# A two-layer decoder trunk on one core: sums of halves moved from GpSimd to VectorE, vectors and masks made at the start, a shared port in the emission's model

## The chip, the cores and the metric

One NeuronCore of a Trainium2 chip runs the whole kernel. The metric is device time in microseconds of one execution. TensorE (PE) multiplies matrices, VectorE (DVE), ScalarE (ACT) and GpSimd (POOL) work elementwise, and SyncE (SP) issues nearly all the DMAs. Each engine runs its own instructions strictly in the order in which they were written, and waits at the first one whose inputs aren't there.

## The reference

`x` is 512 tokens by 1024 features in float32. Each of two layers is a half-weighted SwiGLU feed-forward part, a mixer of two branches, and a second feed-forward part:

```python
for l in range(DEPTH):                                   # DEPTH = 2
    x = x + 0.5 * swiglu(rmsnorm(x, n1[l]), w_in1[l], w_out1[l])   # d_ff = 2816
    x = x + hybrid_mixer(rmsnorm(x, nm[l]), ...)
    x = x + 0.5 * swiglu(rmsnorm(x, n2[l]), w_in2[l], w_out2[l])

def swiglu(h, w_in, w_out):
    gate, up = jnp.split(h @ w_in, 2, axis=-1)
    return (jax.nn.silu(gate) * up) @ w_out
```

The mixer projects `h` onto the inputs of branch A (a gated DeltaNet of 8 heads: short convolution, chunks of 64 tokens with a triangular solve, and a state carried from chunk to chunk) and of branch B (stick-breaking attention of 8 heads), and onto gates. Both branches go through their own 1024x1024 projection, are gated, added, and projected by `w_out`.

## The kernel before, in words

Everything is kept transposed, features on partitions, 512 tokens along the free axis. Matmuls run in float32r with each operand split into a high and a low part: ACT makes the high part of a weight chunk (`wh`), DVE the low part (`wl<-raw,wh`), and a product is three matmuls, high by high, low by high and high by low (`mm3`). An ordinary projection gives matmuls named `pf`.

**Feed-forward part.** The first four column units of the hidden layer ("c" in the `PLAN`) are ordinary products. The rest is made in nine quads ("s"): a quad takes four weight blocks b11, b21, b22, b12 and forms seven products of halves instead of eight. For that each quad needs four sums of weight blocks (`sums` and `last_sum`: in the trace `s<-sraw`, `sraw<-sraw` twice, and `sraw<-s,sraw`, each 128x1024), and the part needs, once, four sums of halves of the normalised activations `xs` (`halves`: `sx<-xs` twice, `xs<-xs`, `sx<-xs,sx`). All of these run on GpSimd. Each sum is the raw form of one further weight operand, so ACT and DVE then split it (`wl<-sraw`, `wl<-s`; `th`, `tl<-sx`). The down projection ("d", matmuls `pf<-hp`) stands between the quads; its first columns come ahead of quad 0. `hp` is the split hidden activation. Split weights live in rings of four buffers in this part (three in the mixer), so a new one can be made when PE is through with the oldest.

**Mixer.** A string `ORDER` says which projection comes when (D and S for the branches, G and Z for gates, B for the projection of branch B, E for the end of the first stage). The DeltaNet runs in four pairs of heads. A pair is a chain: scores, a blocked inverse (`pp`, `pt`), then four rounds over the tokens (`dn_recur`: PE `pa`, DVE `rhs`, PE `py`, ACT `y` and `yw`, PE `po`, DVE `s`), then the norm of the heads (`dn_out`: `osq`, `dsc`, scaling on ACT, transposes `oT` on PE). Such chains are put in between the matmuls of projections, so that PE has work while it waits for the other engines.

**What sets the order.** The program is emitted by Python code in which a model (`Weave`, with a cost for each engine, `COST`) keeps a clock. After each projection matmul `tick` lets every chain whose inputs the model holds to be ready emit its next step. `idle(engine)` puts a step off while the model's engine is busy, `until` runs chains up to a condition, and `drain` runs all of them out. The order that results on PE, ACT, DVE and POOL is final. At "E" `drain` runs whatever chain is left, with no projection matmul between its steps.

**The start.** `load_x` loads x in five DMAs, transposes it block by block (`xps`, into a ring of three PSUM buffers with the tag "dp", which `vp` and `adt_ps` share), and starts the first two column units. Only the gain of the first norm is loaded ahead of x (`column`). All other vectors per feature (`vt`, turned by a transpose `vp` and a copy), the row of decay parameters (`adt_row`, spread by the matmul `adt_ps`) and the masks are made by `more_constants`, a chain that is released 20 us (model time) later and must be done before quad 0.

Of the kernel before, what the change touches and what calls it, by code (L numbers as in the profile page):

```python
# [74 lines left out]
class Weave:  # L75
# [13 lines left out]
    def __init__(self, nc):  # L89
        self.t = 0.0  # L90
        self.cur = 0.0
        self.free = dict.fromkeys(("vector", "scalar", "gpsimd", "sync", "dma"), 0.0)
        self.writes = {}
# [38 lines left out]
    def charge(self, engine, op, outs, ins, func=None):  # L132
# [20 lines left out]
        else:  # L153
# [182 lines left out]
class Trunk:  # L336
# [46 lines left out]

    def column(self, name, ap):
        for _ in self.columns(name, ap):
            pass

    def columns(self, name, ap):

        nc = self.nc  # L390
        rows = ap.shape[0]
        dst = self.cst.tile([P, rows], F32, name="v_" + name)
        for r0 in range(0, rows, P):
            n = min(P, rows - r0)
            t = self.stat.tile([P, P], F32, tag="sq", bufs=SQ, name="vt")
            nc.scalar.dma_start(t[:n, :], ap[r0:r0 + n, :])
            yield self.weave.landed(t)
            ps = self.dps.tile([P, SEQ], F32, tag="dp", name="vp")
            nc.tensor.transpose(ps[:, :n], t[:n, :], self.ident[:n, :n])
            nc.vector.tensor_copy(dst[:, r0:r0 + n], ps[:, :n])  # L400
        self.vcol[name] = dst

    def constants(self):
        nc = self.nc
        self.vcol = {}
        self.ident = self.select("ident", ALU.is_equal, 0, 1, -1)
        self.ones = self.cst.tile([P, P], F32, name="ones")
        nc.gpsimd.memset(self.ones, 1.0)
        self.eps = self.cst.tile([P, 1], F32, name="eps")
        nc.gpsimd.memset(self.eps, EPS)  # L410

    def more_constants(self, vecs, a_log, dt_bias):
        nc = self.nc
        c = self.cst
        for name, ap in vecs:
            yield from self.columns(name, ap)
            yield 1000
        t = self.stat.tile([P, P], F32, tag="sq", bufs=SQ, name="gt")
        self.select("gt", ALU.is_gt, 0, 1, -1, out=t)
        self.m_gt = c.tile([P, P], F32R, name="m_gt")  # L420
        nc.scalar.copy(self.m_gt, t)
        self.m_le = self.select("m_le", ALU.is_ge, 0, -1, 1)
# [12 lines left out]
        yield 2000  # L435

        n = DEPTH * HEADS
        row = c.tile([1, 2 * n], F32, name="adt_row")
        nc.scalar.dma_start(row[:, 0:n], a_log.rearrange("(o l) h -> o (l h)", o=1))
        nc.scalar.dma_start(row[:, n:2 * n], dt_bias.rearrange("(o l) h -> o (l h)", o=1))  # L440
        yield self.weave.landed(row)
        ps = self.dps.tile([P, SEQ], F32, tag="dp", name="adt_ps")
        nc.tensor.matmul(ps[:, :2 * n], self.ones[0:1, :], row, start=True, stop=True)
# [3 lines left out]
        nc.scalar.activation(self.nea, self.adt[:, 0:n], AF.Exp)  # L447
        nc.vector.tensor_scalar(self.nea, self.nea, -1.0, None, op0=ALU.mult)
        self.sbg = c.tile([P, DEPTH], F32, name="sbg")
# [11 lines left out]

    def load_x(self, x, gain):

# [3 lines left out]
        with self.pool("xin", 1) as xin:  # L467
            self.column(*gain)
# [75 lines left out]
    def finish_norm(self):  # L544

        nc = self.nc
        nc.scalar.preload_act_table_set("natural_log_exp_and_others")
        ps = self.dps.tile([P, SEQ], F32, tag="dp", name="ssps")
        nc.tensor.matmul(ps, self.ones, self.ssq, start=True, stop=True)
        y = self.stat.tile([P, SEQ], F32, tag="r", name="r")  # L550
        tmp = self.stat.tile([P, SEQ], F32, tag="sq", bufs=SQ, name="rtmp")
        nc.scalar.activation(tmp, ps, AF.Ln, scale=1.0 / D, bias=self.eps[:, 0:1])
        nc.scalar.activation(y, tmp, AF.Exp, scale=-0.5)
        nc.vector.tensor_scalar(tmp, ps, 1.0 / D, EPS, op0=ALU.mult, op1=ALU.add)
        nc.vector.tensor_mul(tmp, tmp, y)
# [231 lines left out]
    def sums(self, q):  # L787
# [9 lines left out]
        nc.gpsimd.tensor_tensor(t[21], t[11], t[21], op=ALU.subtract)  # L797
        f.events.add("s3")
        yield 0
        while 1 not in f.events:  # L800
            yield 300
        nc.gpsimd.tensor_tensor(t[11], t[0], t[11], op=ALU.subtract)
        f.events.add("s2")
        yield 0

    def last_sum(self, q):
        f, t = self.fours[q], self.fours[q].tiles
        while not f.events >= {2, "s2"}:
            yield 300
        self.nc.gpsimd.tensor_tensor(t[12], t[12], t[11], op=ALU.subtract)  # L810
        f.events.add("s4")
# [3 lines left out]
    def halves(self, hid):  # L815
# [60 lines left out]
    def ffn(self, hid, w_in, w_out, finish, first=None):  # L876
# [127 lines left out]
        for item in PLAN:  # L1004
            if item[0] == "d" and later is None:
# [721 lines left out]
def hybrid_trunk(ctx, tc, x, ffn1_norm, ffn1_w_in, ffn1_w_out, mix_norm, w_in, dn_conv_w, dn_a_log,  # L1727
# [9 lines left out]
    def gains(name, l):  # L1737
# [3 lines left out]
        mybir.EngineType.PE, mybir.EngineType.Activation, mybir.EngineType.DVE, mybir.EngineType.Pool}))  # L1741
    T.constants()
    T.begin_norm(gains("n1", 0))
    first = T.load_x(x[0], ("n1", rows(ffn1_norm)))
    T.weave.spawn(T.weave.after("constants", T.more_constants([
        ("nm", rows(mix_norm)), ("n2", rows(ffn2_norm)),
        ("conv", dn_conv_w.rearrange("l t (k p) -> (l t k) p", p=P)),
        ("dno", dn_out_norm), ("sbq", sb_q_norm), ("sbk", sb_k_norm),
    ], dn_a_log, dn_dt_bias)), 20000)

# [49 lines left out]
```

## Time and profile before

| | us |
|---|---|
| median of 3 runs (2808.15 to 2808.47) | 2808.41 |
| the profiled execution | 2805.78 |
| its span (first to last instruction) | 2803.9 |
| PE busy | 2750.8 |
| DVE busy | 1998.8 |
| ACT busy | 1466.4 |
| POOL busy | 681.7 |

The span is what the trace covers; 1.9 us of the profiled execution lie around it. Times in the rows are counted from the span's start. A row of a timeline has start, duration, engine, line of the helper that issued it, operation, output and inputs, shapes, count, and in brackets how long the engine had been idle and what released it. All instructions go through one helper, so the line is always the same and rows are told apart by the names of their tiles. "PEclk" is TensorE's granted clock as a share of 2.4 GHz.

### The profile page before, as it was taken

What the parts mean: (1) busy time and instruction counts of PE and PEld (TensorE: products, weight loads), DVE (VectorE), ACT (ScalarE), POOL (GpSimd) and SP (SyncE); (2) the same over time, 40 slices, a digit from 0 to 9 for tenths busy, and PEclk for the clock granted to TensorE, in tenths of its full rate; (3) what the DMA queues carried; (4) which work ended last, traced back from release to release, by engine and by line L of the source; (5) the groups of instructions that cost most, each with busy time, mean ns of one, the idle gap of its engine ahead of it and who ended that gap; (6) DMA issues with size and microseconds to landing.
All of it is one profiled execution on the core that took longest, in us unless ns stands there. A gap on an engine that the chain in (4) does not pass through costs nothing.

```text
span 2803.9 us, 44397 instructions
## 1 busy us (share of the span) xinstructions
PE 2750.8 (98%) x17230; PEld 2441.1 (87%) x17230; DVE 1998.8 (71%) x2994; ACT 1466.4 (52%) x2955; POOL 681.7 (24%) x400
## 2 busy tenths in 40 slices
PE   8999999999999999999999999999999999999999
PEld 6899988888888887999979999889988888889998
DVE  6877576986787556867578675778878765588664
ACT  4544346767664544534445344468675745445333
POOL 5444120100100044523145341210001002355330
PEclk9999999999999999999999999999999999999999
DMA  5333143322335654333143331323323358433332
GB/s 152 102 106 105 49 123 89 95 78 83 96 97 180 222 170 134 102 100 112 50 132 97 103 116 56 113 81 86 102 80 96 104 158 291 137 95 106 102 94 64
DMA packets 438034, 312.47 MB, mean 111 GB/s; under 512 B 31562, under 2 KB 408128, under 8 KB 437824
## 3 DMA queue, kind: packets, MB, share of 16 engines
q1 hardware_dynamic: 437488, 309.51, 36.9%
q8 instruction: 135, 2.21, 0.3%
q14 instruction: 75, 0.61, 0.1%
q10 hardware_dynamic: 336, 0.13, 0.0%
HBM read 276.03 MB, written 33.55 MB: 110 GB/s over the span
## 4 chain that ended last, share of the span: by engine, by line
PE 79%; DVE 10%; issue 4%; ACT 3%; POOL 2%; DMA 1%; SPq 0%; DVEq 0%; POOLq 0%; ACTq 0%
PE pf L279 51%; PE pq L279 15%; PE ps L279 7%; DVE wl L279 3%; ACT u L279 1%; DVE itmp L279 1%; DVE sbs L279 1%; PE sbo_ps L279 1%; DVE qkv L279 1%; POOL t L279 1%; DVE it L279 1%; PE z_ps L279 1%; PE pa L279 1%; PE at_ps L279 0%; PE pp L279 0%
## 5 line engine op out<-in xcount | busy, mean ns | idle before, releaser
L279 DVE TENSOR_TENSOR wl<-raw,wh 128x1024 fp32r<-128x1024 f32 (+2 forms) x351 | 430.8, 1228 | 138.4 <-ACT wh L279 135.7
L279 ACT ACTIVATE wh<-raw 128x1024 fp32r<-128x1024 f32 (+2 forms) x352 | 336.9, 959 | 300.6 <-PE pf L279 149.9
L279 PE MATMUL pf<-xh,wl 128*128 128x512 f32 (+1 forms) x1312 | 486.1, 371 | 5.3 <-DVE wl L279 5.3
L279 PE MATMUL pf<-xh,wh 128*128 128x512 f32 (+1 forms) x1312 | 487.0, 371 | 0.2 <-DVE t L279 0.2
L279 PE MATMUL pf<-xl,wh 128*128 128x512 f32 (+1 forms) x1312 | 486.7, 371 | 0.0
L279 PE MATMUL pf<-hp,wh 128*128 128x512 f32 x1408 | 439.3, 392 | 2.1 <-DVE hp L279 1.1
L279 DVE TENSOR_TENSOR wl<-sraw,wh 128x1024 fp32r<-128x1024 f32 x216 | 377.3, 1757 | 64.3 <-ACT wh L279 64.3
L279 PEld LDWEIGHTS pf<-hp,wh 128*128 128x128 f32 x1408 | 264.6, 189 | 58.3 <-DVE hp L279 2.2
L279 ACT ACTIVATE wh<-sraw 128x1024 fp32r<-128x1024 f32 x216 | 228.3, 1057 | 133.7 <-PE pf L279 102.1
L279 PEld LDWEIGHTS pf<-xh,wl 128*128 128x128 f32 x1312 | 248.0, 189 | 48.1 <-DVE wl L279 8.9
L279 PE MATMUL pf<-hp,wl 128*128 128x512 f32 x704 | 276.0, 392 | 7.6 <-DVE wl L279 7.6
L279 PEld LDWEIGHTS pf<-xl,wh 128*128 128x128 f32 x1312 | 248.0, 189 | 39.1 <-issue 1.2
L279 PEld LDWEIGHTS pf<-xh,wh 128*128 128x128 f32 x1312 | 248.0, 189 | 38.6 <-issue 1.1
L279 POOL TENSOR_TENSOR sraw<-sraw 128x1024 f32<-128x1024 f32 x72 | 212.2, 2963 | 246.1 <-DVE wl L279 189.9
L279 PE MATMUL pq<-th,wh 128*128 128x256 f32 x864 | 244.9, 283 | 3.0 <-ACT u L279 3.0
L279 PE MATMUL pq<-th,wl 128*128 128x256 f32 x864 | 244.6, 283 | 0.3 <-DVE wl L279 0.3
L279 PE MATMUL pq<-tl,wh 128*128 128x256 f32 x864 | 244.5, 283 | 0.0
L279 PE MATMUL pf<-wh,xh 128*128 128x256 f32 x768 | 225.3, 293 | 0.0
L279 PE MATMUL pf<-wl,xh 128*128 128x256 f32 x768 | 217.3, 283 | 0.0
L279 PE MATMUL pf<-wh,xl 128*128 128x256 f32 x768 | 216.9, 282 | 0.0
L279 DVE SCALAR_TENSOR_TENSOR x<-pf,x 128x512 f32<-128x512 f32 x128 | 87.7, 687 | 156.9 <-PE pf L279 156.7
L279 PEld LDWEIGHTS pq<-th,wh 128*128 128x128 f32 x864 | 165.8, 192 | 3.9 <-ACT u L279 3.8
(1090 smaller groups left out, 6275.3 us busy)
## 6 DMA issues: line engine op xcount, KB each, us to landing
sraw<-in_ffn_w_in_dram SPq DMA_DIRECT2D x144, 512.0 KB, 3.6
raw<-in_w_in_dram SPq DMA_DIRECT2D x144, 512.0 KB, 3.9
raw<-in_ffn_w_out_dram SPq DMA_DIRECT2D x96, 384.0 KB, 3.4
raw<-in_ffn_w_in_dram SPq DMA_DIRECT2D x32, 512.0 KB, 3.9
raw<-in_ffn_w_out_dram SPq DMA_DIRECT2D x32, 256.0 KB, 2.8
gsp<-gt SPq DMA_DIRECT2D x32, 256.0 KB, 2.7
of<-osp SPq DMA_DIRECT2D x32, 256.0 KB, 3.9
raw<-in_w_branch_b_dram SPq DMA_DIRECT2D x16, 512.0 KB, 4.0
```

What stands on the lines that cost most here:

```text
L279: return f(*args, **kw)
```

## The change

Four things are changed.

1. The 144 sums of weight blocks and the 16 sums of halves of activations are issued on VectorE. Ahead of each, `idle("vector", ...)` is asked.
2. `constants` issues all loads of vectors at once, ahead of x: five from ACT's queue (16, 128, 64, 16 and 16 rows of 128), five from POOL's (the three small vectors and the two halves of `adt_row`), and then makes the masks on POOL. Behind block 1 of x, `load_x` now has two transposes, one copy, the matmul `adt_ps` and its copy, `sbg`, and ACT's copy of one mask. The gate before quad 0 is gone, and one small exponential is made in the first `finish_norm`.
3. The model knows a port that VectorE (operations with two wide inputs in SBUF) and GpSimd (with one or more) share: such an operation starts when the port is free, and holds it to its end. As this model sets the order of everything, the whole program is emitted in another order.
4. `finish_norm` waits 800 ns of model time before it emits the sum over features (`ssps`).

```diff
@@ class Weave, charge
-            end = self.free[engine] = max(self.free[engine], need) + fixed + per * n
+            wide = sum(a.space != bass.MemoryType.PSUM and m > 1 for a, m in zip(ins, sizes[len(outs):]))
+            start = max(self.free[engine], need)
+            if wide >= {"vector": 2, "gpsimd": 1}.get(engine, 9):
+                start = max(start, self.port)
+                self.port = start + fixed + per * n
+            end = self.free[engine] = start + fixed + per * n
@@ constants
+        for group in (vecs[:1], vecs[1:]):
...
+                    (nc.scalar if rows > 2 else nc.gpsimd).dma_start(
+                        tiles[at // P][at % P:at % P + m, :], ap[r:r + m, :])
...
+        nc.gpsimd.dma_start(self.adt_row[:, 0:n], a_log.rearrange("(o l) h -> o (l h)", o=1))
+        nc.gpsimd.dma_start(self.adt_row[:, n:2 * n], dt_bias.rearrange("(o l) h -> o (l h)", o=1))
@@ load_x
+            self.turn_vectors()
             for k in range(KD + 4):
+                if k == 2:
+                    self.turn_vectors()
+                    self.more_constants()
@@ finish_norm
+        yield 800
         ps = self.dps.tile([P, SEQ], F32, tag="dp", name="ssps")
@@ sums, last_sum (each of the four)
-        nc.gpsimd.tensor_tensor(t[0], t[21], t[22], op=ALU.add)
+        yield from self.weave.idle("vector", LO_WAIT)
+        nc.vector.tensor_tensor(t[0], t[21], t[22], op=ALU.add)
@@ halves
-            nc.gpsimd.tensor_tensor(raw[i], a, b, op=ALU.subtract)
+            yield from self.weave.idle("vector", 1500)
+            nc.vector.tensor_tensor(raw[i], a, b, op=ALU.subtract)
@@ ffn
-            if item == ("s", 0, 1):
-                self.weave.until(lambda: self.weave.done("constants"))
```

At the start of the program PE's order before was this (`vp` turns the first gain, each `xps` group is a block of x, `pf` the first column unit):

```order
L279 MATMUL vp<-ident,vt 128x16
L279 MATMUL xps<-ident,xin_116 128x128 x4
L279 MATMUL xps<-ident,xin_118 128x128 x4
L279 MATMUL xps<-ident,xin_122 128x128 x4
L279 MATMUL pf<-xh,wh 128x512
```

and it is now:

```order
L285 MATMUL vp<-ident,vt 128x16
L285 MATMUL xps<-ident,xin_141 128x128 x4
L285 MATMUL xps<-ident,xin_143 128x128 x4
L285 MATMUL vp<-ident,vt 128x128
L285 MATMUL vp<-ident,vt 128x102
L285 MATMUL adt_ps<-adt_row,ones 128x32
L285 MATMUL xps<-ident,xin_147 128x128 x4
L285 MATMUL pf<-xh,wh 128x512
```

Two transposes and `adt_ps` have moved ahead of block 2 of x. Later in the same part the single `vp` and `adt_ps` matmuls between the `pf<-hp` are gone.

At the start of the second feed-forward part of layer 0, around the first columns of the down projection, VectorE's order before was this (`wl<-raw` 128x512 are the weights of those columns, `tl<-sx` splits the sums that POOL had made, `t` and `hp` belong to the last column unit):

```order
L279 TENSOR_TENSOR hp<-t,hp 128x512
L279 TENSOR_TENSOR wl<-raw,wh 128x512
L279 TENSOR_TENSOR t<-pf,r 128x512
L279 TENSOR_TENSOR tl<-sx,th 128x1024
L279 TENSOR_TENSOR wl<-raw,wh 128x512
L279 TENSOR_TENSOR tl<-sx,th 128x1024
L279 TENSOR_TENSOR t<-pf,t 128x512
L279 TENSOR_TENSOR tl<-sx,th 128x1024
L279 TENSOR_TENSOR hp<-t,hp 128x512
```

and it is now:

```order
L285 TENSOR_TENSOR sraw<-sraw 128x1024
L285 TENSOR_TENSOR hp<-t,hp 128x512
L285 TENSOR_TENSOR sx<-xs 128x1024
L285 TENSOR_TENSOR t<-pf,r 128x512
L285 TENSOR_TENSOR wl<-raw,wh 128x512
L285 TENSOR_TENSOR sx<-xs,sx 128x1024
L285 TENSOR_TENSOR t<-pf,t 128x512
L285 TENSOR_TENSOR wl<-raw,wh 128x512
L285 TENSOR_TENSOR tl<-sx,th 128x1024
L285 TENSOR_TENSOR hp<-t,hp 128x512
```

The sums stand among VectorE's own work, and both weights of the first two columns now stand ahead of the first `tl<-sx`.

At the end of the mixer's first stage in layer 0, where the last DeltaNet pair finishes, PE's order before was this (`pf<-sph` and `pf<-spl` are the projection of branch B; 16 more of its matmuls follow before the first `oT`, and 3 between the two groups of `oT`):

```order
L279 MATMUL pa<-s,qkv 128x128 x4
L279 MATMUL pf<-spl__9386,wh 128x512
L279 MATMUL py<-rhs,tt 128x128
L279 MATMUL pf<-sph__9385,wl 128x512
L279 MATMUL py<-rhs,tt 128x128
L279 MATMUL pf<-sph__9394,wh 128x512
L279 MATMUL po__9908<-y,at 128x128
L279 MATMUL po__9911<-y,at 128x128
L279 MATMUL pf<-spl__9395,wh 128x512
L279 MATMUL pf<-sph__9394,wl 128x512
```

and it is now:

```order
L285 MATMUL py<-rhs,tt 128x128 x2
L285 MATMUL po__9892<-yw,kw 128x128
L285 MATMUL po__9892<-y,at 128x128
L285 MATMUL po__9898<-yw,kw 128x128
L285 MATMUL po__9898<-y,at 128x128
L285 MATMUL pa<-s,qkv 128x128 x4
L285 MATMUL py<-rhs,tt 128x128 x2
L285 MATMUL po__9926<-y,at 128x128
L285 MATMUL po__9929<-y,at 128x128
L285 MATMUL oT<-ident,qkv 128x128 x8
L285 MATMUL pf<-xh,wh 128x512
```

No projection matmul stands between these steps any more: the pair's inverse comes when nine matmuls of the projection of B are left, and from the first round's `po` on the chain stands alone, until the next projection (`pf<-xh`) behind `oT`. The order is the same at this place in layer 1.

## Rows read from the trace of the kernel before

**Rows 1.** The page: engines' busy time; the chain of waits by engine.

```profile
PE 2750.8 (98%) x17230; PEld 2441.1 (87%) x17230; DVE 1998.8 (71%) x2994; ACT 1466.4 (52%) x2955; POOL 681.7 (24%) x400
PE 79%; DVE 10%; issue 4%; ACT 3%; POOL 2%; DMA 1%; SPq 0%; DVEq 0%; POOLq 0%; ACTq 0%
```

**Rows 2.** PE's waits: what it waited for, us in total, times, longest.

```profile
PE pf L279 <- DVE wl L279: 12.9, 10, 2.6
PE ssps L279 <- POOL ssq L279: 4.1, 3, 1.7
...
PE vp L279 <- DMA vt<-in_dn_out_norm_dram: 3.7, 1, 3.7
PE z_ps L279 <- DVE qkl L279: 3.6, 2, 1.8
...
PE pk L279 <- ACT qkv L279: 3.1, 4, 1.3
PE pq L279 <- ACT u L279: 3.0, 4, 0.9
...
PE adt_ps L279 <- DMA adt_row<-in_dn_dt_bias_dram: 1.2, 1, 1.2
PE pf L279 <- DVE hp L279: 1.1, 2, 0.6
PE pf L279 <- ACT hp L279: 1.0, 2, 0.5
```

**Rows 3.** Windows: us, busy time by engine, PEclk, DMA share, GB/s.

```profile
75.00:79.00 4.00, 4.00 (x13) 3.09 (x12) 2.40 (x5) 1.00 (x2) 0.00 (x0) 0.57 0.56 165
2491.82:2495.86 4.04, 4.04 (x11) 2.96 (x11) 4.04 (x6) 2.81 (x6) 0.00 (x0) 0.58 0.64 189
```

**Rows 4.** Timeline of the start, PE and DVE.

```profile
9.38 1.09 PE L279 MATMUL xps<-ident,xin 128*128 128x128 f32 x4 [3.56 <-DMA xin<-in_x_dram]
10.65 0.68 DVE L279 COPY x<-xps 128x512 f32<-128x512 f32 x1
```

**Rows 5.** Timelines at the second feed-forward's start, layer 0: DVE, POOL, PE.

```profile
1101.74 2.35 DVE L279 TENSOR_TENSOR tl<-sx,th 128x1024 fp32r<-128x1024 f32 x1 [1.65 <-ACT th L279]
1104.02 2.83 DVE L279 TENSOR_TENSOR wl<-raw,wh 128x512 fp32r<-128x512 f32 x1
1106.78 1.21 DVE L279 TENSOR_TENSOR tl<-sx,th 128x1024 fp32r<-128x1024 f32 x1
...
1110.85 0.68 DVE L279 TENSOR_TENSOR wl<-raw,wh 128x512 fp32r<-128x512 f32 x1
...
1102.98 3.33 POOL L279 TENSOR_TENSOR sx<-xs,sx 128x1024 f32<-128x1024 f32 x1
...
1106.90 0.50 PE L279 MATMUL pf<-hp,wl 128*128 128x512 f32 x1 [2.49 <-DVE wl L279]
```

**Rows 6.** Tile view of the sums: duration ns min/median/max, first and last start.

```profile
L279 DVE TENSOR_TENSOR wl<-sraw,wh x216: 1207/1225/3420, 88.4 to 2754.8; 128x1024 fp32r<-128x1024 f32 x108
...
L279 POOL TENSOR_TENSOR sraw<-sraw x72: 2397/2881/3414, 58.4 to 2741.8; 128x1024 f32<-128x1024 f32 x72
```

**Rows 7.** Window of one quad of products, same columns as rows 3.

```profile
160.16:180.32 20.16, 20.16 (x170) 20.16 (x170) 18.10 (x15) 10.30 (x14) 11.20 (x5) 1.00 0.38 116
```

**Rows 8.** Timeline of PE at the mixer's end, layer 0.

```profile
915.42 0.39 PE L279 MATMUL pf<-spl__9443,wh 128*128 128x512 f32 x1
915.65 0.60 PE L279 MATMUL py<-qkv,tt 128*128 128x128 f32 x4
...
927.60 0.49 PE L279 MATMUL po__9911<-y,at 128*128 128x128 f32 x2
...
932.61 0.60 PE L279 MATMUL oT<-ident,qkv 128*128 128x128 f32 x4
933.75 0.61 PE L279 MATMUL oT<-ident,qkv 128*128 128x128 f32 x4
```

**Rows 9.** Window between the last `po` and `oT`, same columns as rows 3.

```profile
927.98:932.61 4.63, 4.63 (x21) 3.66 (x21) 2.82 (x18) 4.20 (x23) 0.00 (x0) 1.00 0.14 57
```

More of the change, by code (lines that the diff above doesn't have):

```diff
@@ L92, in __init__ @@
         self.free = dict.fromkeys(("vector", "scalar", "gpsimd", "sync", "dma"), 0.0)
+        self.port = 0.0
         self.writes = {}
@@ L382, in select, with constants @@
         return t
[L384 to L388, printed above, removed]
+    def constants(self, vecs, a_log, dt_bias):
         nc = self.nc
[L391 to L401, printed above, removed]
@@ L403, in constants @@
-    def constants(self):
-        nc = self.nc
+        c = self.cst
         self.vcol = {}
         self.ident = self.select("ident", ALU.is_equal, 0, 1, -1)
-        self.ones = self.cst.tile([P, P], F32, name="ones")
+        self.ones = c.tile([P, P], F32, name="ones")
         nc.gpsimd.memset(self.ones, 1.0)
-        self.eps = self.cst.tile([P, 1], F32, name="eps")
+        self.eps = c.tile([P, 1], F32, name="eps")
         nc.gpsimd.memset(self.eps, EPS)
[L412 to L421, printed above, removed]
+        self.vrows = []
@@ new lines, in constants @@
+        for group in (vecs[:1], vecs[1:]):
+            n = sum(ap.shape[0] for _, ap in group)
+            dst = c.tile([P, n], F32, name="v_" + group[0][0])
+            tiles = [self.stat.tile([P, P], F32, tag="sq", bufs=SQ, name="vt") for _ in range(0, n, P)]
+            at = 0
+            for name, ap in group:
+                r, rows = 0, ap.shape[0]
+                self.vcol[name] = dst[:, at:at + rows]
+                while r < rows:
+                    m = min(rows - r, P - at % P)
+                    (nc.scalar if rows > 2 else nc.gpsimd).dma_start(
+                        tiles[at // P][at % P:at % P + m, :], ap[r:r + m, :])
+                    r, at = r + m, at + m
+            self.vrows.append((dst, tiles, n))
@@ L434, in more_constants, with turn_vectors @@
                                     pattern=[[-1, 8], [1, 32]], channel_multiplier=0)
-        yield 2000
+    def turn_vectors(self):
+        nc = self.nc
+        dst, tiles, n = self.vrows.pop(0)
+        ps = self.dps.tile([P, SEQ], F32, tag="dp", name="vp")
+        for i, t in enumerate(tiles):
+            m = min(P, n - i * P)
+            nc.tensor.transpose(ps[:, i * P:i * P + m], t[:m, :], self.ident[:m, :m])
+        nc.vector.tensor_copy(dst, ps[:, :n])
+    def more_constants(self):
+        nc = self.nc
+        c = self.cst
         n = DEPTH * HEADS
[L438 to L441, printed above, removed]
+        self.m_gt = c.tile([P, P], F32R, name="m_gt")
+        nc.scalar.copy(self.m_gt, self.gt)
         ps = self.dps.tile([P, SEQ], F32, tag="dp", name="adt_ps")
-        nc.tensor.matmul(ps[:, :2 * n], self.ones[0:1, :], row, start=True, stop=True)
+        nc.tensor.matmul(ps[:, :2 * n], self.ones[0:1, :], self.adt_row, start=True, stop=True)
         self.adt = c.tile([P, 2 * n], F32, name="adt")
@@ L553, in finish_norm @@
         nc.scalar.activation(y, tmp, AF.Exp, scale=-0.5)
+        if self.gt is not None:
+            n = DEPTH * HEADS
+            nc.scalar.activation(self.nea, self.adt[:, 0:n], AF.Exp)
+            nc.vector.tensor_scalar(self.nea, self.nea, -1.0, None, op0=ALU.mult)
+            self.gt = None
         nc.vector.tensor_scalar(tmp, ps, 1.0 / D, EPS, op0=ALU.mult, op1=ALU.add)
@@ L801, in sums @@
             yield 300
-        nc.gpsimd.tensor_tensor(t[11], t[0], t[11], op=ALU.subtract)
+        yield from self.weave.idle("vector", LO_WAIT)
+        nc.vector.tensor_tensor(t[11], t[0], t[11], op=ALU.subtract)
         f.events.add("s2")
@@ L809, in last_sum @@
             yield 300
-        self.nc.gpsimd.tensor_tensor(t[12], t[12], t[11], op=ALU.subtract)
+        yield from self.weave.idle("vector", LO_WAIT)
+        self.nc.vector.tensor_tensor(t[12], t[12], t[11], op=ALU.subtract)
         f.events.add("s4")
@@ L1741, in hybrid_trunk @@
         mybir.EngineType.PE, mybir.EngineType.Activation, mybir.EngineType.DVE, mybir.EngineType.Pool}))
-    T.constants()
-    T.begin_norm(gains("n1", 0))
[L1744 to L1749, printed above, removed]
+    T.constants([
+        ("n1", rows(ffn1_norm)), ("conv", dn_conv_w.rearrange("l t (k p) -> (l t k) p", p=P)),
+        ("nm", rows(mix_norm)), ("n2", rows(ffn2_norm)),
+        ("dno", dn_out_norm), ("sbq", sb_q_norm), ("sbk", sb_k_norm),
+    ], dn_a_log, dn_dt_bias)
+    T.begin_norm(gains("n1", 0))
+    first = T.load_x(x[0])
     for l in range(depth):
```

12 lines of the change are left out of this document (7 added, 5 removed).

## The prediction, made before the result

> **What bounds the kernel now.** I read the page first. TensorE is busy for 2750.8 of 2803.9 us and holds 79% of the chain that ended last [rows 1]. So the change can win only what PE loses: 53.1 us in which it stands idle, and what it loses at a lower granted clock. VectorE is busy 71% of the time, so it has room over the whole, and the question is where. Then I read what PE waited for [rows 2]. The list is short: VectorE's low parts of weights 12.9 us in ten waits, loads of vectors 3.7 and 1.2, the sum for the norm 4.1, ScalarE's `u` 3.0, hidden activations `hp` 2.1 in four, and some chains of the mixer. Last I read the windows behind the longest waits [rows 3]: the granted clock is 0.57 and 0.58 on average there, which is a stretch mostly at 1.2 instead of 2.4 GHz, right behind idle times of 3.7 and 2.5 us. PE works the whole of both windows, so they cost it 4.00 x 0.43 = 1.7 us and 4.04 x 0.42 = 1.7 us more.
>
> **The vectors and masks.** The transposes of the small vectors and `adt_ps` stood between matmuls of the first feed-forward part, where PE waited for their loads: 3.7 and 1.2 us [rows 2], and 1.7 at the low clock behind the first [rows 3]. They go: -6.6 us. What is moved costs something at the start. `xps` of block 2 took PE up at 9.38, after 3.56 us of waiting for x [rows 4]. Now it uses a PSUM buffer of the ring of three that `vp` and `adt_ps` have gone through too, so it waits for the copy of block 1, which ended at 10.65 + 0.68 = 11.33 [rows 4]: +2.0 us. The two transposes, `adt_ps` and their copies lie in the wait that is there already. The lower bound is 0 (PE waits later in this part for VectorE anyway, and part of the delay can vanish in those waits), the upper one is 3.7, if a load on POOL's queue is as late as the one of [rows 2] was; I take 2.0, since the copy's end is a row and the late load is not. The ten loads at the start together are small, and x's own loads come from SP, past which nothing is moved.
>
> The Trainium skill speaks against this placement: SBUF — State Buffer, in the box on the "DVE blocks DMA" trap under "SBUF: two separate sides", says that a DMA issued from GpSimd's queue needs GpSimd to write its descriptors, which it can't while VectorE holds the port that they share; a transfer of some 620 ns then took some 3100 ns. By that, and called an estimate, five such loads in a row could land 5 x 2.5 = 12 us late and hold `adt_ps`, and the start term would be about 8 instead of 2. No row here shows a load from POOL's queue.
>
> **The sums on VectorE, first columns.** GpSimd's sums and VectorE's operations with two inputs slow each other. At the start of the second feed-forward part, `sx<-xs,sx` ran 3.33 us on POOL, and beside it `tl<-sx` took 2.35 and `wl<-raw` 128x512 took 2.83 us, where the same forms a little later take 1.21 and 0.68 [rows 5]. These two lost 1.1 and 2.2 us, and PE waited 2.49 us for that `wl` [rows 5]. Three of the four parts begin like this; the longest such wait is 2.6 [rows 2]. In the new order both weights stand ahead of the first `tl`, and of the sums only one of 128x1024 lies between them, about 1.2 us by the same form. So the wait goes: 3 x 2.5 = 7.5, the 1.7 at the low clock behind the last of them [rows 3], and the waits for `hp` behind them, 2.1 [rows 2]: 11.3 in all. I take 10, because the sums now stand in VectorE's queue ahead of `t` and `hp`; the bounds are 4 (one more late step in each part) and 11.3.
>
> **The sums on VectorE, quads.** In the quads PE is the bound. A quad of seven products takes 20.16 us and PE works for all of it, with VectorE busy 18.1 in 15 instructions and POOL 11.2 in its four or five sums [rows 7]. There is no wait to win. VectorE gets four more operations per quad. At the median of the form, 1.22 us [rows 6], they are 4.9 us. In exchange its seven `wl` of a quad lose what the lock cost them: the largest takes 3.42 where the smallest takes 1.21, and a sum on POOL takes 2.9 [rows 6]. Eleven operations of 1.22 and seven of about 0.68 [rows 5] make 18.2 us of 20.16, as much as before. I take 0, as the ring of four split weights lets VectorE run ahead of PE; the price if a sum comes late is a rival's, below.
>
> **The norm.** `ssps` waited for POOL's sum of squares three times, 4.1 in all, of which the longest is 1.7 [rows 2], at the very start of the program. The other two, 1.2 each, stand behind the mixers, and there `ssps` now comes some four matmuls of 0.23 later: -2.0 (0 to -2.4). At the program's start it has its old place, and stays. The waits for `u`, 3.0 in four [rows 2], lie in the first quads where the port was contended: half goes, -1.5 (0 to -3.0).
>
> **The new order at the mixer's end.** This is the part which the list of edits doesn't show. With the port in the model, the last DeltaNet pair's chain is emitted later, when the projection of branch B is nearly used up; `drain` then emits the rest of it alone. In the order before, 39 more matmuls of projections stood inside the chain between its first `py` and the second group of `oT` than now stand there. One of them takes 915.65 - 915.42 = 0.23 us [rows 8], so they hid 39 x 0.23 = 9.0 us of the chain's 933.75 - 915.65 = 18.1 [rows 8]. Those matmuls now run earlier, and PE stands idle in their place. If the chain were as long as before, the loss would be 9.0. It becomes shorter where a matmul of the projection stood ahead of a step that was ready: about 0.5 us in each of three rounds, and about 0.9 at the end, where ScalarE, busy for 4.20 of the 4.63 us between the last `po` and `oT` [rows 9], made a copy for the projection too. I take 9.0 - 2.4 = 6.6 per layer. The end alone leaves PE idle for about 4 us, longer than the waits of [rows 3], behind which 1.7 us were lost at the low clock: 8.3 per layer. The order is the same in both layers: +16.6 us. The bounds are 2 x 5.5 = 11 (1 us more hidden in each layer, no fall of the clock) and 2 x (9.0 + 1.7) = 21.4.
>
> **The sum.** -6.6 - 10.0 - 2.0 - 1.5 + 2.0 + 16.6 = -1.5 us. On the profiled execution, 2805.78 (span 2803.9 and 1.9 around it), that is 2804.3; the median of the runs shown is 2.6 above the profiled one, so 2808.41 - 1.5 = **2806.9**. The middle of the mixer, where every chain has moved by a few matmuls, I leave at 0: its waits, such as 3.6 for `qkl` and 3.1 for `qkv` [rows 2], come from chains that are as long as before.
>
> **Rivals.** (a) *The new order is better than that in the mixer.* A model that knows the port puts chains where they are really ready: the 3.6 and 3.1 us [rows 2] go, and the drained chain costs its lower bound, 11 instead of 16.6. For it: those waits follow operations on VectorE. Against it: the same model placed the last pair where nothing hides it. 2806.9 - 6.7 - 5.6 = 2794.6: faster. (b) *VectorE becomes late in the quads: slower.* It is in order, so a sum that waits for its weight block's load holds the `wl` behind it, while on POOL such a wait held nothing else. Place: the sum that opens the next quad, 36 times. With 18.2 of 20.16 us filled [rows 7], it decides once a quad's sums wait for more than 2.0 us in all; 2.4 us would cost PE 0.4 each, 36 x 0.4 = 14.4: 2821.3. Against it: the ring of four weights, which buys some products of time. (c) *The first columns don't win.* If `t` or a sum, waiting on another engine, holds the second column's `wl` as long as the port did, the 10 us stay: 2816.9. This is also the case in which the change doesn't do what it says, for POOL keeps its `t<-t,r` and its sums of squares, and the port with them. (d) *A load from POOL's queue is late at the start* and PE waits 3.7 us more, as it did for `vt` [rows 2]: 2810.6.
>
> **Chances.** About 0.2% (5.6 us) is what a measurement of this kernel can tell from no change, so the same is 2802.8 to 2814.0. My forecast has 0.47, with its own range of 2800 to 2814, of which 0.11 lies below 2802.8 and 0.02 above; (a) 0.21, faster; (b) 0.13, slower; (c) 0.14, of which 0.11 slower; (d) 0.05, the same. That gives faster 0.32, the same 0.42, slower 0.26. The range reaches to (a) and to (b), each at its price: 2794 to 2821.
>
> **What would show it.** The list of PE's waits without `vp` and `adt_ps` loads, without the three waits of 2.5 us for `wl` ahead of the first `pf<-hp`, and with a new one of about 4 us at `oT` and smaller ones at `po`, `py` and `pa` in each mixer, all with the last pair; the granted clock near 1.2 GHz behind `oT`; block 2 of x some 2 us later. Waits of PE for `wl<-sraw` or `wl<-s` inside the quads would show (b), waits for `wl` ahead of `pf<-hp` (c). I am wrong if PE's idle time at the drained chains is under 10 us in all, or if POOL's absence doesn't bring `tl` and `wl` to 1.2 and 0.7 us.

## The result

The changed kernel takes 2832.31 us (median of six runs, 2830.89 to 2833.90) where the kernel before, run beside it, takes 2808.34 (2807.34 to 2810.01): a ratio of 1.0085, with a 95% interval of 1.0072 to 1.0098. I had forecast 2806.9, with a range to 2821: the change is slower by 24.0 us, and outside the range. The profiled execution took 2833.59 us (span 2831.9), 27.8 more than that of before.

The page of the changed kernel: engines' busy time, and the chain by engine (before: [rows 1]).

```profile
PE 2773.0 (98%) x17225; PEld 2447.4 (86%) x17225; DVE 2005.3 (71%) x3148; ACT 1467.7 (52%) x2953; POOL 239.2 (8%) x245
...
PE 77%; DVE 15%; ACT 4%; issue 2%; DMA 1%; POOL 1%; DVEq 0%; ACTq 0%; POOLq 0%; SPq 0%
```

POOL has lost two thirds of its work and VectorE's total has hardly moved: its 154 further instructions take the place of what it lost beside POOL's sums. But PE is busy 22 us longer for the same products, and idle 59 us instead of 53. Two things count as busy here and do no more work: stretches at the lower granted clock, and chains of small matmuls. In the drained chain below, PE is idle for only 0.84 us between the first `py` and the last `po`, though hardly any projection matmul is left there.

What PE waited for in the changed kernel (us, times, longest; before: [rows 2]):

```profile
PE oT L285 <- ACT qkv L285: 7.8, 2, 3.9
PE pf L285 <- DVE wl L285: 7.3, 8, 3.2
...
PE ssps L285 <- POOL ssq L285: 2.3, 3, 1.7
PE pf L285 <- ACT wh L285: 2.2, 4, 0.8
```

The two waits at `oT`, one in each mixer, are new. The waits for `wl` have shrunk from 12.9, and those for the small vectors in mid-stream, for `hp` and for `u` are gone.

Where the 27.8 us come from is read by stage: the start of the first matmul of each kind of projection on PE, and the differences of these starts. All kernels of this study do the same work in each stage, but for the one with a letter of `ORDER` moved. The stages come from the one profiled execution of each kernel; in us, good to about 0.1, and the last row ends with PE's last matmul. "First stage" is the mixer up to the projection of B, "B and gates" is that projection and the next two gates, where the last DeltaNet pair ends. The rest of each mixer takes 87.0 in every kernel.

| stage | before | changed | no port rule | sums alone | vectors alone |
|---|---|---|---|---|---|
| to the first `pf` | 10.1 | 12.8 | 13.6 | 10.2 | 12.8 |
| first feed-forward, layer 0 | 366.7 | 360.2 | 356.9 | 357.6 | 363.1 |
| first stage, layer 0 | 500.9 | 508.3 | 502.2 | 502.4 | 501.8 |
| B and gates, layer 0 | 91.3 | 102.1 | 91.3 | 91.3 | 91.3 |
| second feed-forward, layer 0 | 353.0 | 349.7 | 347.0 | 347.9 | 353.4 |
| first feed-forward, layer 1 | 352.8 | 349.1 | 346.3 | 346.3 | 353.1 |
| first stage, layer 1 | 500.9 | 512.9 | 501.0 | 501.0 | 501.0 |
| B and gates, layer 1 | 91.2 | 103.4 | 91.3 | 91.3 | 91.3 |
| second feed-forward, layer 1 | 359.1 | 355.2 | 352.8 | 353.3 | 359.6 |

The last three columns are experiments below. Before against changed: the feed-forward parts win 6.5, 3.3, 3.7 and 3.9 us, 17.4 in all; the start loses 2.7; the mixers lose 7.4 + 10.8 and 12.0 + 12.2, 42.4 in all. The sum is +27.7.

The mixer's end in layer 0, timeline of PE (start, us, ..., idle before; before: [rows 8]), and windows of 5 us behind it (PEclk is the third number from the end):

```profile
931.54 0.60 PE L285 MATMUL py<-qkv,tt 128*128 128x128 f32 x4
931.90 0.47 PE L285 MATMUL pf<-sph__9410,wl 128*128 128x512 f32 x1
...
936.11 0.49 PE L285 MATMUL po__9854<-yw,kw 128*128 128x128 f32 x2 [0.34 <-ACT yw L285]
...
943.34 0.49 PE L285 MATMUL po__9929<-y,at 128*128 128x128 f32 x2
947.71 2.53 PE L285 MATMUL oT<-ident,qkv 128*128 128x128 f32 x8 [3.88 <-ACT qkv L285]
```

```profile
945.00:950.00 5.00, 2.29 (x9) 1.47 (x9) 2.00 (x14) 4.22 (x19) 0.00 (x0) 0.80 0.00 0
950.00:955.00 5.00, 5.00 (x20) 4.11 (x20) 1.22 (x1) 3.73 (x5) 0.00 (x0) 0.85 0.70 238
...
2345.00:2350.00 5.00, 1.12 (x6) 0.60 (x5) 2.93 (x18) 4.19 (x23) 0.00 (x0) 0.75 0.01 3
2350.00:2355.00 5.00, 5.00 (x16) 3.81 (x16) 1.23 (x1) 4.59 (x8) 0.00 (x0) 0.57 0.45 150
```

From the first `py` to the first `oT` the chain takes 947.71 - 931.54 = 16.2 us. In the kernel before it took 932.61 - 915.65 = 17.0 [rows 8] with 37 matmuls of a projection among its steps, 8.5 us at 0.23 each. (17 of them stood up to the last `po` and 20 behind it; the count of 16 more ahead of `oT`, given with the order above, should be 18.) Hidden or not, its length is nearly the same. The first two windows lose 5 x 0.20 + 5 x 0.15 = 1.75 us at the low clock. The last two are the same place in layer 1: they lose 5 x 0.25 + 5 x 0.43 = 3.4 us, of which an estimated 0.8 lie in the wait itself, which ends at 2349.11.

In layer 1, where PE's order is the same, three more stretches fell to a lower clock in the first stage, behind waits of 0.55, 2.09 and 0.46 us:

```profile
2055.00:2060.00 5.00, 4.45 (x32) 3.61 (x32) 3.58 (x5) 2.85 (x10) 0.10 (x1) 0.74 0.39 108
2190.00:2195.00 5.00, 5.00 (x32) 5.00 (x31) 2.43 (x6) 3.33 (x22) 0.00 (x0) 0.66 0.56 161
2245.00:2250.00 5.00, 5.00 (x25) 4.34 (x24) 0.73 (x2) 2.39 (x9) 0.00 (x0) 0.66 0.36 105
```

They cost 5 x (0.26 + 0.34 + 0.34) = 4.7 us, and 0.4 more in the window that follows the first (clock 0.92). The two layers' first stages, 512.9 and 508.3, differ by 4.6, and waits of like length stand in layer 0. That the falls make this difference is borne out by the kernel with the port rule alone, below: there the clock falls once in the first stage of layer 0 (800.00 to 805.00 reads 0.66, a loss of 1.7 us) and not in layer 1, and the stages take 509.8 and 508.1.

### The profile page after: what moved, and what is told of

Same layout as the page of the kernel before. It is cut to its first block, busy times and chain, and to the rows that moved or that the text cites. A ratio compares the mean times of both kernels' runs of the same rounds, so it can differ in the third digit from the quotient of the medians.

```text
span 2831.9 us, 44146 instructions
## 1 busy us (share of the span) xinstructions
PE 2773.0 (98%) x17225; PEld 2447.4 (86%) x17225; DVE 2005.3 (71%) x3148; ACT 1467.7 (52%) x2953; POOL 239.2 (8%) x245
## 4 chain that ended last, share of the span: by engine, by line
PE 77%; DVE 15%; ACT 4%; issue 2%; DMA 1%; POOL 1%; DVEq 0%; ACTq 0%; POOLq 0%; SPq 0%
PE pf L285 48%; PE pq L285 15%; PE ps L285 7%; DVE wl L285 3%; DVE itmp L285 2%; DVE sbs L285 2%; DVE qkv L285 1%; DVE it L285 1%; ACT u L285 1%; DMA raw<-in_ffn_w_out_dram 1%; PE pa L285 1%; ACT wh L285 1%; DVE u L285 1%; DVE dsc L285 1%; PE sbo_ps L285 1%
## 5 line engine op out<-in xcount | busy, mean ns | idle before, releaser
L285 DVE TENSOR_TENSOR wl<-raw,wh 128x1024 fp32r<-128x1024 f32 (+2 forms) x351 | 404.4, 1153 | 141.5 <-ACT wh L285 138.9
L285 DVE TENSOR_TENSOR wl<-sraw,wh 128x1024 fp32r<-128x1024 f32 x216 | 264.0, 1222 | 51.3 <-ACT wh L285 51.3
L285 PEld LDWEIGHTS pq<-tl,wh 128*128 128x128 f32 x864 | 165.8, 192 | 0.2
```

Source lines behind the costliest of these rows:

```text
L285: return f(*args, **kw)
```

## The experiments

### Each part alone

The theory after the two traces: the edits themselves win as the feed-forward rows of the table say, and the port rule in the emission's model, which sets the mixers' order, loses the rest. The rivals: the sums cost VectorE time in the quads, or the loads cost time at the start.

**Without the port rule.** The changed kernel less this:

```diff
-            if wide >= {"vector": 2, "gpsimd": 1}.get(engine, 9):
-                start = max(start, self.port)
-                self.port = start + fixed + per * n
```

> The changed kernel without the shared port in the emission's model; sums on VectorE, vectors at the start and the delay ahead of the norm stay. Built like this, the mixers' order is that of before. Theory: the port rule alone made the mixers longer (42.4 us in both, from the two traces), so this gives 2832.3 - 42.4 = about 2790; up to 2804 if the first columns of the feed-forward parts win only in the order that the rule makes. Rival: the sums on VectorE or the loads at the start cost the time, then it stays above 2808.

Measured: 2784.11 us (2781.91 to 2785.32), 0.9915 of the kernel before (0.9900 to 0.9929). The rule costs 48.2 us, and without it the change is a gain of some 24. The column "no port rule" shows both mixers back within 1.3 us of the times of before, and the feed-forward parts 2.4 to 3.3 us faster each than with the rule, which the theory had not held.

**The port rule alone.** The kernel before, with those lines:

> The kernel before with the port rule in the emission's model and nothing else; sums on GpSimd. Theory: the mixers lose what they lose in the changed kernel, 2808.3 + 42.4 = about 2851, less some us if the feed-forward parts are emitted better by the rule. Rival, that the rule hurts only in company with the other edits: 2803 to 2813.

Measured: 2858.84 us, 1.0182 (1.0167 to 1.0197). The mixers' four rows are 509.8, 104.1, 508.1 and 103.2, against 508.3, 102.1, 512.9 and 103.4 in the changed kernel. The rule needs no company to do harm. With the sums on GpSimd it also made the feed-forward parts slower than before (369.8, 356.4, 355.5, 362.1), where I had expected a few us of gain.

**The sums alone.** The kernel before, with the sums on VectorE behind `idle("vector", ...)` (one of the five places):

```diff
-        nc.gpsimd.tensor_tensor(t[0], t[21], t[22], op=ALU.add)
+        yield from self.weave.idle("vector", LO_WAIT)
+        nc.vector.tensor_tensor(t[0], t[21], t[22], op=ALU.add)
```

> The kernel before with the 160 sums on VectorE and nothing else. Theory: the waits ahead of the first columns of three feed-forward parts go, about 3 x 2.5 us, 1.7 at the low clock, and 1 to 4 of small waits: 2795 to 2800. Rival, VectorE late in the quads (0.4 us in each of 36): 2808 or more.

Measured: 2782.78 us, 0.9913 (0.9896 to 0.9929): the sums alone win 25 us, where I had expected 8 to 13. The tile view shows why there is no late VectorE in the quads (ns min/median/max; before: [rows 6]):

```profile
L279 DVE TENSOR_TENSOR wl<-sraw,wh x216: 1212/1220/1228, 81.9 to 2730.3; 128x1024 fp32r<-128x1024 f32 x108
...
L279 DVE TENSOR_TENSOR sraw<-sraw x72: 1209/1225/1228, 56.8 to 2717.1; 128x1024 f32<-128x1024 f32 x72
```

The maximum of `wl<-sraw` has gone from 3420 to 1228 ns, and a sum costs 1.2 us on VectorE where it cost 2.9 on POOL. VectorE's slow `wl` are gone, and with them each of the three starts of 32.0 us (from the first `pf<-hp` to the next quad) is down to 27.7, with no wait of PE in it. One thing was not in the edit. In this trace, timeline of PE, the small vectors' transposes and `adt_ps` have no wait ahead of them any more:

```profile
76.13 0.22 PE L279 MATMUL vp<-ident,vt 2*128 2x2 f32 x1
81.72 0.22 PE L279 MATMUL vp<-ident,vt 2*128 2x2 f32 x1
85.95 0.22 PE L279 MATMUL vp<-ident,vt 2*128 2x2 f32 x1
87.92 0.40 PE L279 MATMUL adt_ps<-adt_row,ones 1*128 1x32 f32 x2
```

The loads are still made in mid-stream, but in the new order their turn comes when they have landed. So the waits that I had given to the vectors' edit, 6.6 us, went with the sums already.

The delay ahead of the norm has no run of its own, but the traces tell it apart. The two waits of 1.20 us for `ssq` behind the mixers are still 1.20 in the kernel with the sums alone, and 0.31 in the changed kernel and in the one without the port rule, which have the delay: 1.8 us in all.

**The vectors alone.** The kernel before, with `constants`, `turn_vectors` and `more_constants` of the changed one:

> The kernel before with vectors and masks made at the start and nothing else. Theory: the loads' stalls and the low clock behind them go, -6.5, and the start costs +2.7, as in the trace of the changed kernel: -3.8, about 2804.5. Rival, that freed waits come back as waits for the first sums (still on GpSimd): 2807 to 2809.

Measured: 2807.02 us, 0.9999 (0.9990 to 1.0009): no change, as the rival had it. By stage, the first feed-forward part wins 3.6 of the 6.5 us that I had expected, the start costs 2.7, and the first stage of layer 0 takes 0.9 longer. What is missing of the 6.5 came back as another wait. Timelines of PE, DVE and POOL at the first down columns of layer 0:

```profile
72.50 0.73 PE L282 MATMUL pf<-hp,wh 128*128 128x512 f32 x2 [1.57 <-ACT wh L282]
74.84 0.77 PE L282 MATMUL pf<-hp,wl 128*128 128x512 f32 x1 [1.61 <-DVE wl L282]
...
63.85 6.75 DVE L282 TENSOR_TENSOR tl<-sx,th 128x1024 fp32r<-128x1024 f32 x2
...
66.14 3.38 POOL L282 TENSOR_TENSOR sx<-xs,sx 128x1024 f32<-128x1024 f32 x1
```

Two `tl` took 6.75 us beside POOL's sums, and PE waited 3.2 us for the weights behind them. In the kernel before, the stall at the load had covered this: it is the wait with which the other three feed-forward parts begin [rows 5], and in this part it was hidden under the worse one.

### Which part of the mixer, and where else

**A projection ahead of E.** The changed kernel with one letter of `ORDER` moved, so that the last pair has matmuls to stand among:

```diff
-ORDER = "DSDDDDGDSDSDDDDDSGSGSZSDSZSDDDSDGDSDDDGDDZDGZSGGZGZCGGGBBBBBBBBEZGGZGG"
+ORDER = "DSDDDDGDSDSDDDDDSGSGSZSDSZSDDDSDGDSDDDGDDZDGZSGGZGZCGGGBBBBBBBBZEGGZGG"
```

> The changed kernel with one letter of ORDER moved: one Z projection comes ahead of E, so the last DeltaNet pair is emitted among its matmuls again (8 of them are left between the last po and oT, where 20 were before and none in the changed kernel). The rest of the mixers keeps the changed order. Theory: the drained chain costs 10.0 and 10.7 us in its stage and 0.8 and 1.5 of low clock behind it; filled but for the end, where 12 matmuls of 0.23 are missing per layer, some 5.5 remain and 17 go: 2832.3 - 17 = about 2815. Rival, that the chain's steps cost in any company: no change, 2830 to 2834.

Measured: 2821.94 us (2819.24 to 2823.35), 10.4 less than the changed kernel, where I had expected 17. "B and gates" takes 97.6 and 98.0 instead of 102.1 and 103.4. What is left is at the end of the chain (timeline of PE, and the window behind it):

```profile
949.04 2.38 PE L285 MATMUL oT<-ident,qkv 128*128 128x128 f32 x8 [2.04 <-ACT qkv L285]
...
950.00:955.00 5.00, 5.00 (x15) 3.56 (x16) 1.27 (x2) 4.41 (x8) 0.00 (x0) 0.66 0.77 251
```

The chain is as long as ever (its first `py` is at 932.73, so 16.3 us to `oT`); a wait of 2.04 us remains since the 8 matmuls were used up, the eight transposes stand in one group, and 1.7 us are lost at the low clock behind it. I had counted the missing matmuls only. So the chain costs what isn't hidden of it, and the clock fell here behind a wait of 2.04 us.

**The rule in the mixers only, and outside them only.** A flag switches the lines off at the start of `mixer` and on at its end, or the other way round:

```diff
+            if self.use_port and wide >= {"vector": 2, "gpsimd": 1}.get(engine, 9):
```

> The changed kernel with the port rule of the model switched on in the mixers only. Theory: 2784.1 (no port rule) plus what the mixers of the changed kernel lose against those without it, 6.1 + 10.0 + 0.8 and 11.9 + 10.6 + 1.5: about 2825. Rival, that the loss comes from an order that the feed-forward parts leave behind: near 2784.

> The changed kernel with the port rule of the model switched on outside the mixers only. Theory: the first columns of the down projection wait again (2.5, 2.4, 1.9 and 2.1 us by stage in the two traces, with and without the rule) and some first quads too: 2784.1 + 9 = 2790 to 2794. Rival, the rule is harmless there and its cost lies in the mixers alone: 2784.

Measured: 2820.61 us in the mixers only, 2797.76 outside only. Against 2784.11 without the rule these are 36.5 and 13.7, together 50.2, where the whole rule costs 48.2: the two parts add up nearly. The first falls some 4 us short of the 2825 that I had expected, the second costs 4 us more than the 2794 at most. In the first trace both first stages take about 509 us, so the 512.9 of layer 1 doesn't come back with the rule. In the second, 3.5 us of the loss stand in the mixers' first stages (503.7 and 502.9), where the rule was off. The rest stands in the feed-forward parts, for the most part where the weights' splits come late. In the changed kernel, timelines of DVE, PE and ACT at the second feed-forward's start:

```profile
1121.96 0.69 DVE L285 TENSOR_TENSOR wl<-raw,wh 128x512 fp32r<-128x512 f32 x1
...
1122.70 0.50 PE L285 MATMUL pf<-hp,wl 128*128 128x512 f32 x1 [0.72 <-DVE wl L285]
...
1128.28 0.63 ACT L285 ACTIVATE wh<-raw 128x512 fp32r<-128x512 f32 x1 [6.29 <-PE pf L285]
```

The third column's `wl` stands behind `hp`, two `tl` and an `xl`, and PE waits 0.72 us for it; the same three starts take 30.2, 29.7 and 29.9 us with the rule and 27.8 without.

### Is it the rule, or any touch of the model?

The first stages of the changed kernel lost 6.1 and 11.9 us against the kernel without the rule, with more than a dozen waits of 0.2 to 2.1 us, for `z_ps`, `po`, `pt`, `pk` and `sbo_ps`, none of which stood out. So the last theory: the order comes from a simulation of events in which every step's time decides what comes next, and any touch can draw another order. Four kernels without the full rule, with one number or one half of it changed:

```diff
-    COST = {"tensor": (1, 0.417), "vector": (70, 1.04), "scalar": (100, 0.84), "gpsimd": (120, 1.3)}
+    COST = {"tensor": (1, 0.417), "vector": (70, 1.03), "scalar": (100, 0.84), "gpsimd": (120, 1.3)}
```

> The changed kernel without the port rule (2784.1), with the model's cost of VectorE per element lowered from 1.04 to 1.03, one per cent, and nothing else. The mixers' order becomes another one (the last pair stays among projection matmuls: 22 between the last po and oT). Theory, any touch of the model draws a new order and most draws are worse than the one that the constants of before give: 2786 to 2812 from the first stages of the mixers alone (the rule's own draw cost 6 and 12 us there). Rival, only the port rule itself makes a bad order: 2782 to 2786.

The second has 1.20 there instead of 1.04:

> The changed kernel without the port rule (2784.1), with the model's cost of VectorE per element raised from 1.04 to 1.20. In this order the last pair is again emitted alone, as in the changed kernel. Theory: the drained chain costs its 10 to 11 us and up to 1.5 of low clock per layer whatever made the order, +22, and the first stages another -5 to +20 for the new draw: 2801 to 2826. Rival, the drained chain is only dear behind the port rule: 2784 to 2798.

The third keeps the rule's half in which only GpSimd waits:

```diff
             if wide >= {"vector": 2, "gpsimd": 1}.get(engine, 9):
-                start = max(start, self.port)
-                self.port = start + fixed + per * n
+                if engine == "gpsimd":
+                    start = max(start, self.port)
+                else:
+                    self.port = start + fixed + per * n
```

> The changed kernel with half of the port rule: in the model GpSimd waits for VectorE's operations of two inputs, but VectorE never waits for GpSimd. The mixers' order is a third one, with the last pair among projection matmuls. Theory: without the drained chain (23 us) and with a new draw of the first stages: 2784.1 plus 0 to 20. Rival, the rule as such is right about the hardware and only VectorE's half spoils the order: at or below 2784.

The fourth raises GpSimd's cost per element from 2.1 to 2.4:

> The changed kernel without the port rule (2784.1), with the model's cost of GpSimd per element raised from 2.1 to 2.4. The mixers' order is close to that of before (the last pair among projection matmuls, some chains shifted). Theory of the draws: 2784 to 2800, nearer to 2784 than the orders that are less alike. Rival, only the port rule makes a bad order: 2782 to 2786.

| kernel | median us | first stage, layers 0 and 1 | B and gates, layers 0 and 1 |
|---|---|---|---|
| no port rule | 2784.11 | 502.2, 501.0 | 91.3, 91.3 |
| VectorE 1.03 | 2793.10 | 505.8, 505.8 | 91.8, 91.8 |
| GpSimd 2.4 | 2789.51 | 502.4, 505.2 | 91.8, 91.8 |
| half the rule | 2800.41 | 509.6, 513.0 | 91.3, 91.3 |
| the rule | 2832.31 | 508.3, 512.9 | 102.1, 103.4 |
| VectorE 1.20 | 2843.53 | 522.1, 516.9 | 102.3, 106.4 |

The stages are those of the profiled executions. One per cent on one number of the model costs 9.0 us on the chip; of the 10.6 us between the two profiled executions about 9.5 stand in the mixers and 1.0 in the first feed-forward part. The half of the rule costs 16.3, and in the first stages as much as the whole one. A model that only holds VectorE for slower makes the worst order (above the range that I gave it), and like the rule's it leaves the last pair to the end, where PE waits again for the scaled heads (list of PE's waits, `c2`):

```profile
PE oT L282 <- ACT qkv L282: 16.2, 4, 4.2
```

Two of these four waits, of 3.88 us, stand at the mixers' ends; the other two, of 4.22, are in the first stages. Its clock is the lowest of all: 0.986 on average over the span, where the kernel without the rule has 0.999 and the changed one 0.995. By these shares the low clock takes some 40 us of its span, against 3 and 14, part of it while PE waits.

So the drained chain is no property of the port rule, and the rivals that only the rule makes a bad order fall. All five touched models of the table gave slower orders than the untouched one. Why that one is good is not shown; that its numbers had been chosen for this order is a rival that no run tests.

### A version that beats both

The changed kernel without the port rule, and with the two transposes and `adt_ps` moved from behind block 1 of x to behind the last block; the vectors' rows wait in another ring of buffers meanwhile:

```diff
-                if k == 2:
+                if k == KD:
                     self.turn_vectors()
                     self.more_constants()
```

> The kernel without the port rule (2784.1), with the two transposes, adt_ps and their copies moved from behind block 1 of x to behind the last block, where no block of x waits for their PSUM buffers. Theory: the 2.7 to 3.4 us by which block 2 came late go: 2781. Rival, PE waits later in this part for VectorE anyway and the gain is taken back: 2784.

Measured: 2779.39 us (2775.43 to 2781.10), 0.9893 (0.9878 to 0.9907). Block 2 of x comes early again, behind its own load and nothing else (timeline of PE):

```profile
9.66 1.09 PE L282 MATMUL xps<-ident,xin 128*128 128x128 f32 x4 [3.61 <-DMA xin<-in_x_dram]
```

To the first `pf` it takes 10.4 us where it took 13.6, and the first feed-forward part isn't longer for it (354.8 against 356.9). Against the sums alone (2782.78) the intervals overlap, and so do those against the kernel without the port rule (2784.11). So it isn't shown that the vectors' edit is worth having beside the sums; in one trace of each, the stages up to the first mixer speak for it, 365.2 against 367.8 us.

## Why the prediction was wrong, by its own steps

**What bounds the kernel** held: the change moves what PE loses. A lower clock was forecast for the mixers' ends alone. Without the program's last windows it costs about 12 us in the changed kernel, summed over windows of 5 us, and 3.4 in that of before.

**The vectors and masks**, -6.6 and +2.0. The waits for the loads went from the changed kernel, and the stage of the first feed-forward shows -6.5. But the step put it down to this edit, and the runs show otherwise: alone the edit gives 3.6 in that stage, since the wait for `wl` stood hidden under the stall, and pays 2.7 at the start; and the sums alone removed the stall too. Waits of an engine that works in order can't simply be added up; the next one behind should have been looked for in the rows. The start's mechanism was exact. Block 2 waited for the copy of block 1 (timelines of PE and DVE, changed kernel):

```profile
10.04 0.60 PE L285 MATMUL adt_ps<-adt_row,ones 1*128 1x32 f32 x2 [1.51 <-DMA adt_row<-in_dn_dt_bias_dram]
12.11 1.09 PE L285 MATMUL xps<-ident,xin 128*128 128x128 f32 x4 [1.47 <-issue]
...
11.33 0.68 DVE L285 COPY x<-xps 128x512 f32<-128x512 f32 x1
```

11.33 + 0.68 = 12.01, and `xps` is at 12.11: 2.7 later than before instead of 2.0, for the copy itself came 0.68 later [rows 4], behind the first weights. PE's waits of 1.59 and 1.51 for the loads, the case of rival (d), ended before that copy and cost nothing more.

The Trainium skill's warning on loads from GpSimd's queue (SBUF — State Buffer, "SBUF: two separate sides") did not bear here. Its box speaks of a VectorE that runs in a 2-port performance mode, a condition that the prediction left out. Issues of the changed kernel, KB each and us to landing:

```profile
vt<-in_dn_conv_w_dram ACTq DMA_DIRECT2D x1, 32.0 KB, 5.6
...
adt_row<-in_dn_dt_bias_dram POOLq DMA_DIRECT2D x1, 0.1 KB, 6.1
```

The slowest of POOL's landed 6.1 us after its issue, and one from ACT's queue 5.6: no queue stands out, at a place where VectorE had little to do, so the rule as such isn't refuted. The 8 us that I had estimated by it didn't come.

**The first columns** (-10), the norm (-2.0) and `u` (-1.5). The mechanism held: with POOL's sums gone and no rule, the last three feed-forward parts win 6.0, 6.5 and 6.3 us, 18.8 where these terms sum to 13.5. The norm's part was right (1.8). The waits for `u`, 3.0, went whole and not by half, and with the sums alone no wait is left at the first columns of these three parts. So the terms were too small, and rival (c) is out. The changed kernel got 10.9 of it, since the rule's order gave some back, which no step of the sum had: the new order was weighed at the mixer's end only. In its feed-forward parts the weights of the third column come late, with a wait of some 0.7 us in each part.

**The quads** (0) held. The window of one quad in the changed kernel (columns as in [rows 7]): PE is full, and VectorE does four sums more in no more time.

```profile
157.00:177.16 20.16, 20.16 (x170) 20.16 (x169) 17.84 (x19) 10.54 (x14) 0.00 (x0) 1.00 0.42 124
```

Rival (b), the one for a slower kernel, is out too: it had the right sign for the wrong place.

**The mixer's end** (+16.6). The place and the cause were right, and so was the low clock behind `oT` in layer 0 (1.7 said, 1.75 measured); in layer 1 it cost about 2.6. The time was 10.8 + 12.2 = 23.0. The failed step is the 2.4 us by which the chain was to become shorter when it stood alone. It became 0.8 shorter (16.2 for 17.0): by 0.15 in the rounds up to the last `po`, where 1.5 were said, and by 0.64 behind it, where 0.9 were said. The matmuls among its steps had hardly delayed it; they fitted into its own waits. Waits of 0.57 and 0.91 us ahead of the chain, for the split inputs of the projection of B, had no term. The upper bound, 21.4, was the better value, and still too low. My sign of being wrong, under 10 us of idle time at the drained chains, misled: PE's idle time from the first `py` to `oT` is 0.84 + 3.88 = 4.7 us per layer, 9.4 in all, and the loss is more than twice that, since the page counts most of the chain as busy.

**The middle of the mixer** (0). This is the step that failed most: +7.4 and +12.0. "From chains that are as long as before" is no reason. A chain of the same length costs PE what isn't put between its steps, and that is what an order sets. My own count of hidden matmuls at the mixer's end said so. Windows of the first stage, in the kernel before for layer 0 and in the changed one for both layers (columns as in [rows 3]):

```profile
376.79:877.70 500.91, 493.56 (x3220) 434.64 (x3218) 392.70 (x860) 331.04 (x898) 43.22 (x67) 1.00 0.35 98
...
373.00:881.32 508.32, 497.29 (x3220) 434.34 (x3218) 387.56 (x841) 331.62 (x899) 46.07 (x68) 1.00 0.34 96
1769.18:2282.10 512.92, 501.82 (x3219) 438.52 (x3218) 387.40 (x841) 331.79 (x899) 45.34 (x68) 0.99 0.33 95
```

PE is idle for 7.4 us in the first and for 11.0 and 11.1 in the other two. So 3.7 us of each layer's loss are waits, 5.1 us in layer 1 are the low clock, and the remaining 3 to 4 us lie in work that is counted as busy and takes longer; which steps those are is not shown. Rival (a) had this place with the other sign; a rival in which the first stages lose as much was missing, and with it the range ended too early.

By terms, on the profiled run: start +2.7, first feed-forward -6.5, the other three -10.9, mixer ends +23.0, first stages +19.4, together +27.7.

## What to carry to other kernels

Where a program emits its order from a model, a better model isn't a better order: build the order, and look at each chain of dependent steps for the matmuls that stand between them, in all stages and not at the worst place only. Price a chain at what no longer stands between its steps, and don't count on its becoming shorter when it stands alone. And when a stall is removed, look for the wait that it had covered before counting the gain; the edit that was to remove it may win nothing alone, and another one may remove it by accident.

## What the runs showed of the hardware

The granted clock fell to its lower level, 1.2 GHz, behind short waits of PE among small matmuls, as the windows above show: a window of 5 us at 0.66 lies partly at either level, and the stretch from 2190.60 to 2193.80 reads 0.50. In the changed kernel it fell behind waits of 0.55, 2.09 and 0.46 us in the first stage of layer 1, and behind 2.04 us at the mixer's end with a projection ahead of E. But behind the wait of 2.49 us in the kernel before [rows 5] it did not (window of before, columns as in [rows 3]):

```profile
1105.00:1110.00 5.00, 2.39 (x8) 1.42 (x8) 5.00 (x5) 2.44 (x4) 1.30 (x1) 1.00 0.58 179
```

In layer 0 of the changed kernel the same order ran with like waits at these places (0.54 us, then 1.09 and 0.95 in a row, then 0.46) and without these falls. The length of a wait alone didn't tell whether the clock would fall, and what did is left open here. VectorE's `wl` of 128x1024 were no longer slowed once POOL's large sums had gone: 1212 to 1228 ns over the 216 of one form, where beside the sums the slowest had taken 3420 [rows 6].
